# Branch products in source order on all queues, two low parts on GpSimd, and another plan of the attention

## The chip, the cores and the metric

The kernel runs on one core of a Trainium2 chip. A core has five engines with a queue each: TensorE (PE, matrix products; its weight loads appear as PEld), VectorE (DVE), ScalarE (ACT), GpSimd (POOL) and SyncE (SP, which only issues transfers). A queue is worked off in order, so an instruction that waits holds up all that stand behind it on its engine. The metric is the device time of one execution in microseconds, lower is better; 1533.11 us is the median of three runs of the kernel before.

## The reference

One layer over 1024 latent tokens (channels D = 1024) and 256 context tokens, in float32:

```python
mod = silu(c) @ w_mod + b_mod                 # six vectors: shift, scale, gate, twice
h = x * (1 + scale1) + shift1
proj = h @ w_in + b_in                        # q, k, v of branches A and B, and gate logits
o_a = windowed_attention(...)                 # 8 heads, +-128 tokens and the context, a sink per head
o_b = global_attention(...)                   # 8 heads, all 1280 keys, q and k normalized
g_a, g_b = split(sigmoid(gate_logits), 2)
y = (g_a * (o_a @ w_branch_a) + g_b * (o_b @ w_branch_b)) @ w_out
x = layer_norm(ALPHA * x + gate1 * y)
h = x * (1 + scale2) + shift2
y = conv_ffn(h)                               # up, depthwise convolution, silu, product, down
out = layer_norm(ALPHA * x + gate2 * y)
```

The change is in the attention's plan and in the line that makes `y` from `o_a` and `o_b`, up to the product with `w_out`.

## The kernel before

**Products in three parts.** Every large product is made from operands split into a high part (float32 rounded to the format fp32r) and a low part (what is left). `split` issues both: a copy, by default on ACT or POOL, and a subtraction on DVE or POOL. `mm3` issues three matmuls, high by high, high by low, low by high. In the profile these are lines 374 to 376, the copy on ACT is line 366 and the low part line 371. Tensors are held with channels on the 128 partitions and tokens along the row, in two halves of 512 tokens.

**Stages.** By the trace the projections and gates run to about 322 us, the attention from 322.7 to about 740, the rest of the branch products to 778.9, the product with w_out to 871, the FFN's up part to 1302 and its down part to 1522.

**Attention.** There are 32 units, one for each branch, block of 128 queries and group of four heads; unit 1_3_0 is branch 1 (global), block 3, group 0. A unit's steps: split and turn its queries (qs, qtr, q1), swap halves of them by a transfer (q2), scores (s), row maxima and scaling on DVE (L786), exponentials on ACT (L795), transposes of the probabilities by PE (tr, tiles pt, L840), their high and low parts, and the products with the values (av, L849), high part first and then low. A tile whose index is in `POOLED` is copied by ACT and split on POOL (ptr, hi L1213, lo L1224); the others are split by ACT and DVE (hi L1218, lo L1224). The reciprocal of the softmax sum takes its own way: one row is sent to DRAM (dn, L826) and read back in two transfers that spread it over the partitions (rb, L830). At the end of a unit ACT copies the product out of PSUM (ptra), POOL makes `up` and `ot` from it, multiplies by rb (`tt`, L1249) and splits the result into the attention output O (L866, L863).

**What sets the order.** `graph` makes a list of all these operations with the engine, a cost and a key each, and `plan` gives the order: at each step it takes, from the first `LOOK` of each engine's list, the operation that can start earliest by its account, where `SLACK` allows a later start for a smaller key. `COST` holds for each kind how long it holds the engine and when its result is there, `KEY` the places relative to the unit's number, `FILL` the place of products that fill PE between units: branch A's products (ptb), weight splits (wh, wl) and gate loads (sg). The source then issues each operation in that order, and the queues keep it, because the attention is written under a manual schedule.

Into the plan are also put sums of parts of w_dn that a transfer (sd, L878) and an accumulating transfer issued by POOL (L879) make, and the first halves of the branch B products of f = 0 to 3 (`grp`, with `bm` for the product with the gate).

**Branch products behind attention.** For f = 0 to 3, `rest` loads the second half of the gate, makes the product of the second half of the tokens (`group`, 12 matmuls, tile b, one of two small PSUM buffers `sml`) and multiplies it by the gate on DVE (`gmul`, L1115). For f = 4 to 7, `both` makes both halves (24 matmuls, one of three large buffers) and multiplies on DVE (L1392). `merge` adds branch A's and branch B's parts (DVE, L1372) and splits the sum into mh (ACT) and ml (DVE) for the product with w_out. The weights w_b of two f each are a block; blocks 0 and 1 are split in the plan, block 2 (rwb2, hwb2, lwb2) and block 3 behind it. `wout_start` loads w_out blocks (rwo, hwo, lwo) and the residual z, scaled on POOL (L1368). From the first of these products on, the order was set by a scheduler and not by the source.

Of the kernel before, what the change touches and what calls it, by code (L numbers as in the profile page):

```python
# [7 lines left out]
F32 = mybir.dt.float32  # L8
R32 = mybir.dt.float32r
AF = mybir.ActivationFunctionType  # L10
ALU = mybir.AluOpType
# [6 lines left out]
KT = 8  # L18
# [21 lines left out]
PWB = 5  # L40
DAH = 3
SINK = 640
POOLED, FILL, SUMS = ((0,), (1, 8)), (16.885703, 28.298765), ('ot1', 'ot1')
LOOK, SLACK = 24, (0, 0, 0.031835, 0.0879, 0.031696)
D3AT = (7, 5), (7, 9), (4, 1), (4, 4), (4, 7), (4, 10), (5, 2)
NXS = 5
RAWB = 3
# [38 lines left out]
def plan(ops, rings, free, look, slack):  # L86
# [5 lines left out]
    while any(todo):  # L92
# [25 lines left out]
        for b in o.uses:  # L118
# [25 lines left out]
PRING = "pt", "s", "av"  # L144
RINGS = dict(pt=3, s=2, av=1, qs=1, q1=2, q2=2, p=8, hi=4, lo=4, ptr=2, up=1, ot=1, rb=2, wraw=1, wh=1, wl=1)

KEY = {'qh': -1.21914, 'qt': -1.187093, 'sc': -0.106225, 'scs': (0.233244, 0.27861),
           'scx': -1.945172, 'tr': 0.840531, 'tru': (0.122743, 0.070723),
           'av': 1.36184, 'st': 1.192968, 'out': 0.661224, 'exd': 1.373419, 'st1': 1.769253, 'wb': (27.79832, 29.926055),
           'wg': (31.897283, 33.009176, 33.189585, 33.435465), 'ge': 0.762978, 'gr': 4.580045}  # L150
UNITS = 32


def graph(x, key=KEY, pooled=((3,), (2, 6)), fill=None, ot=("ot0", "ot1")):
    ops, last = [], {}
    def op(kind, k, fn, after=(), takes=(), uses=()):
        e, occ, lat = COST[kind]
        o = Op(e, kind, occ, lat, k, fn, after, takes, uses, kind in PORT)
        ops.append(o)
        return o  # L160
# [21 lines left out]
    for u in range(UNITS):  # L182
# [71 lines left out]
        r = op("rc", kn, lambda u=u, p=pt, b=rb: x.rc(u, p, b), [t], [rb], [pt])  # L254
        dn = op("dn", kn, lambda u=u: x.dn(u), [r], uses=[rb])
        rbd = op("rb", kn, lambda u=u: x.rb(u), [dn], uses=[rb])
        av = Buf("av")
        avo, trs = [], []
        for j, n in enumerate(kt):
# [61 lines left out]
    for f2 in (0, 1):  # L321
        raw = Buf("wraw")
        k = key["wb"][f2]
        a = op("ld", k, lambda f2=f2, r=raw: x.ld(4 + f2, r), [grps[-1]], [raw])
        b_ = op("wh", k + .1, lambda f2=f2, r=raw: x.wh(4 + f2, r, None), [a], uses=[raw])
        c = op("wl", k + .1, lambda f2=f2, r=raw: x.wl(4 + f2, r, None), [b_], uses=[raw])
        for n in (2 * f2, 2 * f2 + 1):
            pt = Buf("pt")
            d = op("sg", UNITS - 1 + .1 * n, lambda f=8 + n: x.sg(f, 0), end)
            e = op("grp", key["wg"][n], lambda f=8 + n, p=pt: x.grp(f, 0, p), [b_, c] + [units[u]["ol"] for u in range(16, 24)], [pt])  # L330
            op("bm", UNITS - .5 + .1 * n, lambda f=8 + n, p=pt: x.bm(f, 0, p), [e, d], uses=[pt])
    op("ld", UNITS - .6, lambda: x.rw(2), end)
    put = {}
    for u0, j0, j1 in ((17, 0, 4), (22, 4, 8), (25, 8, 11)):
# [17 lines left out]
def layer_kernel(  # L352
# [70 lines left out]
    def hput(*names):  # L423
        for n in names:
            hfree.append(hslot.pop(n))
# [686 lines left out]

    def gmul(br, f, hf):
        b = bT[br, f][:, hf * HALF:(hf + 1) * HALF]
        nc.vector.tensor_tensor(out=b, in0=bacc[br, f, hf], in1=b, op=ALU.mult)  # L1115
# [185 lines left out]
    pp.release()  # L1301
    qp.release()

    def rest(f, mk):
        gload(1, f, 1)
        group(1, f, 1, mk(f"b1_{f}_1"))
        gmul(1, f, 1)


    za = tc.alloc_tile_pool(name="za", bufs=1, side="right", reuse_waits="tile")  # L1310
    wq = tc.alloc_tile_pool(name="wq", bufs=1, side="right", reuse_waits="tile")
# [15 lines left out]
    def sml(name, w=512):  # L1327
        return ps3.tile([P, w], F32, tag="sml", name=name, bufs=2)
# [41 lines left out]
    def merge(f):  # L1370
        m = bT[0, f]
        nc.vector.tensor_tensor(out=m, in0=m, in1=bT[1, f], op=ALU.add)  # L1372
        mh, ml = ht(f"mh{f}", dt=R32), ht(f"ml{f}", dt=R32)
        split(m, mh, ml, nc.scalar, nc.vector)
        hput(f"bT0_{f}", f"bT1_{f}")
        mrg.append((mh, ml))

    wb = {2: [wq.tile([P, 8, P], R32, tag="w", name=f"{a}wb2", bufs=4) for a in "hl"]}
    split(rwb[2], *wb[2], nc.scalar, nc.vector)
    hput("rwb2")  # L1380

    def both(f):
        bT[1, f] = ht(f"bT1_{f}")
        nc.sync.dma_start(bT[1, f], sgd[KT + f])
        ps = big(f"b1_{f}")
        w = wb[f // 2]
        for hf in (0, 1):
            for j in range(4):
                k = (f % 2) * 4 + j
                a = O[1, hf, 0, j // 2][:, j % 2], O[1, hf, 1, j // 2][:, j % 2]  # L1390
                mm3(ps[:, hsl(hf)], (w[0][:, k], w[1][:, k]), a, j == 0, j == 3)
        nc.vector.tensor_tensor(out=bT[1, f], in0=ps, in1=bT[1, f], op=ALU.mult)  # L1392

    for f in range(KT):
        if f < 4:
            rest(f, sml)
        else:
            both(f)
        merge(f)
        if f == 3:  # L1400
            wb[3] = weight(w_b[3], "wb3", 8, he=nc.scalar, le=nc.vector, rtag=None)
        if f in (5, 7):
            wout_start(f // 2 - 2, None)
    opool.release()

    post = tc.alloc_tile_pool(name="post", bufs=1, side="left", reuse_waits="tile")
# [789 lines left out]
```

## Time and profile before

| what | value |
|---|---|
| median of the runs (lowest, highest) | 1533.11 us (1532.28, 1533.4) |
| profiled execution | 1533.52 us |
| its span | 1531.7 us |
| busy: PE, DVE, ACT, POOL | 1512.8, 1144.3, 801.2, 772.2 us |
| the largest waits of PE | branch products 4.4 us, attention's av 1.9 and 0.7 us |

A row of a timeline has the start, the duration, the engine, the line, the operation, the output and inputs, and in brackets how long the engine was idle just before and what ended that. SPq is SP's queue. A view of waits has, for each engine and line, what was waited for, the total, the number of times and the longest. Rows that belong to a helper have the helper's line, so the tile's name tells which of its calls it is. A matmul's row is longer than the time to the next, since matmuls are pipelined.

### The profile page before, as it was taken

Reading aid. Unit: us, or ns where it says so; the run is one execution under the profiler, and the core shown is the slowest. Engines: PE = TensorE matmul, PEld = TensorE weight load, DVE = VectorE, ACT = ScalarE, POOL = GpSimd, SP = SyncE. Lnnn points to the kernel's source line nnn. Section 1 sums busy time; section 2 is a strip of 40 time slices with the busy share of each in tenths; the row PEclk is TensorE's granted clock in tenths of the full one; section 3 lists DMA queues with packets and bytes.
Section 4 is the critical chain, followed back from the end, with each engine's and each line's share of the span. In section 5 each row is a group of like instructions: output and inputs, shape, how many; then the busy total and the mean of one; then the engine's idle time right before and its main releaser. Section 6 shows DMA issues by size and latency. Waiting matters only on the chain.

```text
span 1531.7 us, 21972 instructions
## 1 busy us (share of the span) xinstructions
PE 1512.8 (99%) x7652; PEld 1272.2 (83%) x7652; DVE 1144.3 (75%) x1729; ACT 801.2 (52%) x1403; POOL 772.2 (50%) x741
## 2 busy tenths in 40 slices
PE   9999999999999999999899999999999999999997
PEld 7888888889998887888788998888888888888886
DVE  7587847629777776787656898888887787656897
ACT  5422223448987776788232574444444444435533
POOL 0365303428896665685323546666676664021063
PEclk9999999999999999999999999999999999999999
DMA  9667663312445663732471223333344446996723
GB/s 377 235 234 254 212 240 111 97 38 67 118 117 145 174 153 94 161 98 70 139 165 35 96 92 109 110 111 112 111 104 110 110 112 183 377 274 213 247 84 110
DMA packets 112161, 229.73 MB, mean 150 GB/s; under 512 B 13521, under 2 KB 27345, under 8 KB 111954
## 3 DMA queue, kind: packets, MB, share of 16 engines
q1 hardware_dynamic: 97040, 199.72, 39.5%
q0 software_dynamic: 10400, 20.19, 8.6%
q10 hardware_dynamic: 4610, 8.42, 1.5%
q8 instruction: 60, 0.98, 0.3%
q14 instruction: 51, 0.42, 0.1%
HBM read 177.09 MB, written 65.87 MB: 159 GB/s over the span
## 4 chain that ended last, share of the span: by engine, by line
PE 92%; DVE 3%; DMA 1%; POOL 1%; issue 1%; ACT 1%; SPq 0%; DVEq 0%; POOLq 0%; ACTq 0%
PE av L849 7%; PE pt L840 6%; PE g L376 4%; PE g L374 4%; PE g L375 4%; PE p L375 3%; PE p L374 3%; PE p L376 3%; PE s L752 3%; PE s L753 3%; PE c L376 2%; PE d L376 2%; PE a L376 2%; PE d L375 2%; PE a L375 2%; PE c L375 2%
## 5 line engine op out<-in xcount | busy, mean ns | idle before, releaser
L1224 DVE TENSOR_TENSOR lo<-pt,hi 128x512 fp32r<-128x512 f32 x188 | 127.9, 688 | 53.0 <-ACT hi L1218 46.5
L371 DVE TENSOR_TENSOR ld<-rd,hd 128x1024 fp32r<-128x1024 f32 x77 | 97.6, 1285 | 49.2 <-ACT hd L366 47.1
L1218 ACT CAST hi<-pt 128x512 fp32r<-128x512 f32 x188 | 108.3, 582 | 39.9 <-PE pt L840 28.9
L366 ACT CAST hd<-rd 128x1024 fp32r<-128x1024 f32 x77 | 79.5, 1050 | 84.9 <-PE p L376 57.9
L374 PE MATMUL p<-hd 128*128 128x512 f32 x264 | 103.4, 392 | 0.0
L375 PE MATMUL p<-ld,hd 128*128 128x512 f32 x264 | 102.9, 390 | 0.4 <-DVE ld L371 0.4
L849 PE MATMUL av<-hi,VT 128*128 128x512 f32 x236 | 101.4, 431 | 1.9 <-POOL hi L1213 1.9
L376 PE MATMUL p<-hd,ld 128*128 128x512 f32 x264 | 102.9, 390 | 0.0
L849 PE MATMUL av<-lo,VT 128*128 128x512 f32 x236 | 101.8, 434 | 0.7 <-POOL lo L1224 0.7
L376 PE MATMUL g<-hh,wlg 128*128 128x512 f32 x256 | 99.8, 390 | 0.4 <-POOL wlg L371 0.4
L374 PE MATMUL g<-hh,whg 128*128 128x512 f32 x256 | 100.1, 391 | 0.0
L375 PE MATMUL g<-hl,whg 128*128 128x512 f32 x256 | 99.8, 390 | 0.0
L371 POOL TENSOR_TENSOR wlg<-wg,whg 128x512 fp32r<-128x512 f32 x32 | 45.1, 1416 | 106.2 <-ACT whg L366 89.1
L786 DVE TENSOR_SCALAR_CACHE_REDUCE p<-s,cvt,nmc 128x1024 f32<-128x1024 f32 x64 | 85.6, 1337 | 5.6 <-PE s L753 5.3
L840 PEld LDWEIGHTS pt<-ident,p 128*128 128x128 f32 x512 | 63.5, 140 | 17.2 <-ACT rb L822 0.4
L795 ACT ACTIVATE p<-p,nm 128x1024 f32<-128x1024 f32 x64 | 73.9, 1154 | 6.2 <-DVE p L786 5.8
L840 PE MATMUL pt<-ident,p 128*128 128x128 f32 x512 | 76.7, 272 | 0.1
L752 PE MATMUL s<-KL,q 128*128 128x512 f32 (+2 forms) x186 | 74.1, 398 | 0.0
L366 ACT CAST wS<-s 128x512 fp32r<-128x512 f32 x76 | 45.3, 621 | 55.1 <-POOL s L1528 54.3
L753 PE MATMUL s<-KL,q 128*128 128x512 f32 (+2 forms) x186 | 69.7, 374 | 0.0
L371 DVE TENSOR_TENSOR wS<-s,wS 128x512 fp32r<-128x512 f32 x57 | 53.5, 966 | 16.6 <-ACT wS L366 16.6
L366 ACT CAST wA<-ru 128x512 fp32r<-128x512 f32 x57 | 35.5, 623 | 57.7 <-PE d L376 28.8
(436 smaller groups left out, 5026.4 us busy)
## 6 DMA issues: line engine op xcount, KB each, us to landing
wml<-in_wmodT_dram SPq DMA_DIRECT2D x48, 512.0 KB
ru<-in_w_up_dram SPq DMA_DIRECT2D x38, 512.0 KB
rd<-td SPq DMA_DIRECT2D x55, 256.0 KB
rd<-sd SPq DMA_DIRECT2D x44, 256.0 KB
rd<-in_w_dn_dram SPq DMA_DIRECT2D x33, 256.0 KB
wm<-in_wmodT_dram SPq DMA_DIRECT2D x16, 512.0 KB
wg<-in_w_g_dram SPq DMA_DIRECT2D x32, 256.0 KB
q<-q SPq DMA_DIRECT2D x64, 128.0 KB
```

The source lines that it names most:

```text
L366: cast[:] = [nc.scalar.copy(hi, src).ins]
L371: low[:] = [lo_eng.tensor_tensor(out=lo, in0=src, in1=hi.bitcast(F32), op=ALU.subtract).ins]
L374: nc.tensor.matmul(ps, a[0], b[0], start=start, stop=False, skip_group_check=resumed)
L375: nc.tensor.matmul(ps, a[0], b[1], start=False, stop=False, skip_group_check=resumed)
L376: return nc.tensor.matmul(ps, a[1], b[0], start=False, stop=stop, skip_group_check=resumed).ins
L752: nc.tensor.matmul(o, self.q1[:, hs], ks, start=True, stop=False)
L753: nc.tensor.matmul(o, self.q2[:, hs], ks, start=False, stop=stop)
L786: nc.vector.tensor_scalar(out=p if self.br else p[:, self.pad + 1:SINK + 1], in0=self.sv[h], scalar1=self.scale()[:, hs] if self.br else - ...
L840: nc.tensor.transpose(tr[:, h * P:(h + 1) * P], src, ident)
L849: nc.tensor.matmul(self.av, v, self.parts[n][low], start=first, stop=self.left == 0)
L1218: nc.scalar.copy(hi, units[u].parts[n])
L1224: e.tensor_tensor(out=lo, in0=src, in1=hi.bitcast(F32), op=ALU.subtract)
```

## The change

It has two parts.

The plan gets other numbers: `KEY`, `FILL`, `SLACK` (all zero now), tile 6 in place of tile 8 of a global unit on POOL, and a longer time for the reciprocals' way back. The loads of the second halves of branch B's gates for f = 0 to 3 become operations of the plan.

The branch products behind the attention are put under the manual schedule of all five queues, in another source order: the low parts of weight blocks 2 and 3 go to POOL, the low part of a merge is issued one step later (`msplit`), the gate loads of f = 4 to 7 are issued ahead (`later`), block 3 is loaded and split at f = 1, and w_out's first blocks are started ahead of the gate product of f = 5 and 7. Lines of the attention's functions move by two, so L1115 becomes L1117.

```diff
-POOLED, FILL, SUMS = ((0,), (1, 8)), (16.885703, 28.298765), ('ot1', 'ot1')
-LOOK, SLACK = 24, (0, 0, 0.031835, 0.0879, 0.031696)
+POOLED, FILL, SUMS = ((0,), (1, 6)), (16.988136, 27.931), ('ot1', 'ot1')
+LOOK, SLACK = 24, (0, 0, 0, 0, 0)
...
-KEY = {'qh': -1.21914, 'qt': -1.187093, 'sc': -0.106225, 'scs': (0.233244, 0.27861),
+KEY = {'qh': -0.919337, 'qt': -1.197497, 'sc': -0.139853, 'scs': (0.199825, 0.270357),
...
         rbd = op("rb", kn, lambda u=u: x.rb(u), [dn], uses=[rb])
+        rbd.lat = 6.0 if 17 <= u < 30 else 4.2
...
             op("bm", UNITS - .5 + .1 * n, lambda f=8 + n, p=pt: x.bm(f, 0, p), [e, d], uses=[pt])
+            op("sg", UNITS - .5 + .1 * n, lambda f=8 + n: x.sg(f, 1), end)
...
-    def rest(f, mk):
-        gload(1, f, 1)
-        group(1, f, 1, mk(f"b1_{f}_1"))
-        gmul(1, f, 1)
...
         mh, ml = ht(f"mh{f}", dt=R32), ht(f"ml{f}", dt=R32)
-        split(m, mh, ml, nc.scalar, nc.vector)
+        nc.scalar.copy(mh, m)
+        mrg.append((mh, ml))
+
+    def msplit(f):
+        mh, ml = mrg[f]
+        nc.vector.tensor_tensor(out=ml, in0=bT[0, f], in1=mh.bitcast(F32), op=ALU.subtract)
         hput(f"bT0_{f}", f"bT1_{f}")
-        mrg.append((mh, ml))
 
     wb = {2: [wq.tile([P, 8, P], R32, tag="w", name=f"{a}wb2", bufs=4) for a in "hl"]}
-    split(rwb[2], *wb[2], nc.scalar, nc.vector)
+    branch = ExitStack()
+    branch.enter_context(tc.manual_schedule(engines={mybir.EngineType.PE, mybir.EngineType.DVE, mybir.EngineType.SP,
+                                                     mybir.EngineType.Activation, mybir.EngineType.Pool}))
+    split(rwb[2], *wb[2], nc.scalar, nc.gpsimd)
     hput("rwb2")
 
     def both(f):
-        bT[1, f] = ht(f"bT1_{f}")
-        nc.sync.dma_start(bT[1, f], sgd[KT + f])
         ps = big(f"b1_{f}")
...
-        nc.vector.tensor_tensor(out=bT[1, f], in0=ps, in1=bT[1, f], op=ALU.mult)
-
+        return ps
+
+    def later(f):
+        bT[1, f] = ht(f"bT1_{f}")
+        nc.sync.dma_start(bT[1, f], sgd[KT + f])
+
+    for f in (4, 5):
+        later(f)
     for f in range(KT):
         if f < 4:
-            rest(f, sml)
+            group(1, f, 1, sml(f"b1_{f}_1"))
+            gmul(1, f, 1)
+            if f:
+                msplit(f - 1)
+            if f == 1:
+                wb[3] = weight(w_b[3], "wb3", 8, he=nc.scalar, le=nc.gpsimd, rtag=None)
+            if f == 3:
+                later(6)
+                later(7)
         else:
-            both(f)
+            ps = both(f)
+            msplit(f - 1)
+            if f in (5, 7):
+                wout_start(f // 2 - 2, None)
+            nc.vector.tensor_tensor(out=bT[1, f], in0=ps, in1=bT[1, f], op=ALU.mult)
         merge(f)
-        if f == 3:
-            wb[3] = weight(w_b[3], "wb3", 8, he=nc.scalar, le=nc.vector, rtag=None)
-        if f in (5, 7):
-            wout_start(f // 2 - 2, None)
+    msplit(KT - 1)
+    branch.close()
```

Three places show what the queues hold. First DVE from the last gate product inside the plan (ptb11_0) on, before; b1_0_1 is the second half of the branch B product of f = 0, bT0_0 and bT1_0 the parts of branch A and B, and the number at a name's end only tells buffers apart:

```order
L1115 TENSOR_TENSOR bT1_3_8404<-ptb11_0_8591,bT1_3_8404 128x512
L371 TENSOR_TENSOR lwb3_8715<-rwb3_8712,hwb3_8714 128x1024
L1115 TENSOR_TENSOR bT1_0_8370<-b1_0_1_8633,bT1_0_8370 128x512
L1372 TENSOR_TENSOR bT0_0_4909<-bT0_0_4909,bT1_0_8370 128x1024
L371 TENSOR_TENSOR lwo0_8787<-rwo0_8784,hwo0_8786 128x1024
L371 TENSOR_TENSOR ml0_8649<-bT0_0_4909,mh0_8648 128x1024
L1115 TENSOR_TENSOR bT1_1_8381<-b1_1_1_8653,bT1_1_8381 128x512
```

and after, from the same gate product on:

```order
L1117 TENSOR_TENSOR bT1_3_8402<-ptb11_0_8598,bT1_3_8402 128x512
L1117 TENSOR_TENSOR bT1_0_8367<-b1_0_1_8642,bT1_0_8367 128x512
L1369 TENSOR_TENSOR bT0_0_4903<-bT0_0_4903,bT1_0_8367 128x1024
L1117 TENSOR_TENSOR bT1_1_8375<-b1_1_1_8660,bT1_1_8375 128x512
L1376 TENSOR_TENSOR ml0_8658<-bT0_0_4903,mh0_8657 128x1024
L1369 TENSOR_TENSOR bT0_1_4925<-bT0_1_4925,bT1_1_8375 128x1024
L1117 TENSOR_TENSOR bT1_2_8386<-b1_2_1_8685,bT1_2_8386 128x512
```

The low parts lwb3 and lwo0 are gone from between the gate products, and ml0 stands behind the second gate product instead of ahead of it.

Second POOL at the end of unit 1_3_0, before; hi1_3_1_1 and lo1_3_1_1 are the parts of pooled tile 1 of the next unit:

```order
L1242 TENSOR_SCALAR up1_3_0_6741<-ptra1_3_0_6737 64x512
L854 TENSOR_TENSOR ot1_3_0_6746<-ptra1_3_0_6737,up1_3_0_6741 64x256 x2
L1249 TENSOR_TENSOR ot1_3_0_6746<-ot1_3_0_6746,rb1_3_0_6674 128x256
L1213 TENSOR_SCALAR hi1_3_1_1_6769<-ptr1_3_1_1_6761 128x512
L866 TENSOR_SCALAR O1000_5403<-ot1_3_0_6746 128x2x128
L1224 TENSOR_TENSOR lo1_3_1_1_6783<-ptr1_3_1_1_6761,hi1_3_1_1_6769 128x512
L863 TENSOR_TENSOR O1010_5414<-ot1_3_0_6746,O1000_5403 128x2x128
```

and after:

```order
L1215 TENSOR_SCALAR hi1_3_1_1_6763<-ptr1_3_1_1_6747 128x512
L1244 TENSOR_SCALAR up1_3_0_6767<-ptra1_3_0_6754 64x512
L1226 TENSOR_TENSOR lo1_3_1_1_6777<-ptr1_3_1_1_6747,hi1_3_1_1_6763 128x512
L856 TENSOR_TENSOR ot1_3_0_6791<-ptra1_3_0_6754,up1_3_0_6767 64x256 x2
L1251 TENSOR_TENSOR ot1_3_0_6791<-ot1_3_0_6791,rb1_3_0_6670 128x256
L868 TENSOR_SCALAR O1000_5456<-ot1_3_0_6791 128x2x128
L865 TENSOR_TENSOR O1010_5459<-ot1_3_0_6791,O1000_5456 128x2x128
L1215 TENSOR_SCALAR hi1_3_1_6_6841<-ptr1_3_1_6_6826 128x512
L1226 TENSOR_TENSOR lo1_3_1_6_6860<-ptr1_3_1_6_6826,hi1_3_1_6_6841 128x512
```

Tile 1 moved from behind the multiply with rb1_3_0 to ahead of it, and the second pooled tile, now 6, stands right behind the unit's outputs.

Third ACT at the end of the branch products, before; mh6 and mh7 are the high parts of the last merges, hwo1 to hwo3 those of w_out blocks:

```order
L366 CAST hwo1_8864<-rwo1_8862 128x1024
L366 CAST mh3_8708<-bT0_3_5020 128x1024
L366 CAST mh4_8747<-bT0_4_5039 128x1024
L366 CAST mh5_8780<-bT0_5_5160 128x1024
L366 CAST mh6_8825<-bT0_6_5520 128x1024
L366 CAST mh7_8858<-bT0_7_5832 128x1024
L366 CAST hwo2_8889<-rwo2_8887 128x1024
```

and after:

```order
L1371 CAST mh4_8755<-bT0_4_5045 128x1024
L368 CAST hwo0_8786<-rwo0_8784 128x1024
L1371 CAST mh5_8798<-bT0_5_5058 128x1024
L1371 CAST mh6_8829<-bT0_6_5361 128x1024
L368 CAST hwo1_8860<-rwo1_8858 128x1024
L368 CAST hwo2_8892<-rwo2_8890 128x1024
L1371 CAST mh7_8872<-bT0_7_5724 128x1024
```

The high part hwo2 moved from behind mh7 to ahead of it; on DVE lwo2 stands ahead of ml7 in the same way.

More of the change, by code (lines that the diff above doesn't have):

```diff
@@ L145 @@
 RINGS = dict(pt=3, s=2, av=1, qs=1, q1=2, q2=2, p=8, hi=4, lo=4, ptr=2, up=1, ot=1, rb=2, wraw=1, wh=1, wl=1)
-KEY = {'qh': -1.21914, 'qt': -1.187093, 'sc': -0.106225, 'scs': (0.233244, 0.27861),
-           'scx': -1.945172, 'tr': 0.840531, 'tru': (0.122743, 0.070723),
-           'av': 1.36184, 'st': 1.192968, 'out': 0.661224, 'exd': 1.373419, 'st1': 1.769253, 'wb': (27.79832, 29.926055),
-           'wg': (31.897283, 33.009176, 33.189585, 33.435465), 'ge': 0.762978, 'gr': 4.580045}
+KEY = {'qh': -0.919337, 'qt': -1.197497, 'sc': -0.139853, 'scs': (0.199825, 0.270357),
+           'scx': -3.142963, 'tr': 0.868828, 'tru': (0.216182, 0.070723),
+           'av': 1.348883, 'st': 1.265771, 'out': 0.885708, 'exd': 1.273589, 'st1': 1.664154, 'wb': (27.969376, 29.459582),
+           'wg': (31.81419, 33.291489, 33.170198, 33.528645), 'ge': -0.046198, 'gr': 4.26668}
 UNITS = 32
```

## The prediction

> **What bounds the kernel now.** I read the page's busy shares first, then the view of what the tensor engine waited for, then the timelines of the engines around its long waits. The page says that TensorE does the work of nearly the whole span:
>
> ```profile
> PE   1512.8 (99%) x7652; PEld 1272.2 (83%) x7652; DVE 1144.3 (75%) x1729; ACT 801.2 (52%) x1403; POOL 772.2 (50%) x741
> ```
>
> ```profile
> PE b L374 <- DVE bT L1115: 4.4, 2, 2.6
> PE av L849 <- POOL hi L1213: 1.9, 2, 1.7
> PE av L849 <- POOL lo L1224: 0.7, 1, 0.7
> ```
>
> The matmuls themselves stay the same, so only waits can be won. The second fence gives total, number and longest of a wait. Two lie in the branch products (b), the rest in attention (av). Both places by the timelines of PE, first the branch products and the undisturbed steps behind them:
>
> ```profile
> 747.04 0.50 PE L374 MATMUL b<-O,hwb 128*128 128x512 f32 x1 [1.81 <-DVE bT L1115]
> 747.38 0.40 PE L375 MATMUL b<-O,hwb 128*128 128x512 f32 x1
> ...
> 753.10 0.50 PE L374 MATMUL b<-O,hwb 128*128 128x512 f32 x1 [2.59 <-DVE bT L1115]
> 753.44 0.49 PE L375 MATMUL b<-O,hwb 128*128 128x512 f32 x1
> 753.73 0.63 PE L376 MATMUL b<-O,lwb 128*128 128x512 f32 x1
> 754.15 0.63 PE L374 MATMUL b<-O,hwb 128*128 128x512 f32 x1
> ...
> 757.08 0.40 PE L375 MATMUL b<-O,hwb 128*128 128x512 f32 x1
> ...
> 778.64 0.39 PE L376 MATMUL b<-O,lwb 128*128 128x512 f32 x1
> 778.87 0.39 PE L374 MATMUL y<-mh,hwo 128*128 128x512 f32 x1
> ```
>
> An undisturbed matmul starts 0.23 us after the one ahead of it (778.64 to 778.87; over long rows 0.227). After the wait of 2.59 us the ten steps from 753.10 to 757.08 take 3.98 us where ten steps take 2.27: 1.71 us more, and the view by windows shows the granted clock at 0.72 there (first column behind POOL's):
>
> ```profile
> 752.00:758.00 6.00, 4.90 (x14) 3.88 (x15) 5.62 (x7) 2.09 (x2) 1.54 (x2) 0.72 0.58 171
> ```
>
> Who was late is told by the other engines:
>
> ```profile
> 740.42 0.34 SPq L1336 DMA_DIRECT2D rwb<-in_w_b_dram  x1
> ...
> 744.08 1.05 ACT L366 CAST hwb<-rwb 128x1024 fp32r<-128x1024 f32 x1 [8.10 <-DMA rwb<-in_w_b_dram]
> ...
> 745.16 1.23 DVE L371 TENSOR_TENSOR lwb<-rwb,hwb 128x1024 fp32r<-128x1024 f32 x1 [4.64 <-ACT hwb L366]
> 746.31 0.68 DVE L1115 TENSOR_TENSOR bT<-b,bT 128x512 f32<-128x512 f32 x1
> 747.02 1.23 DVE L1372 TENSOR_TENSOR bT<-bT,bT 128x1024 f32<-128x1024 f32 x1
> 749.49 1.41 DVE L371 TENSOR_TENSOR lwo<-rwo,hwo 128x1024 fp32r<-128x1024 f32 x1 [1.24 <-ACT hwo L366]
> 750.82 1.63 DVE L371 TENSOR_TENSOR ml<-bT,mh 128x1024 fp32r<-128x1024 f32 x1
> 752.37 1.28 DVE L1115 TENSOR_TENSOR bT<-b,bT 128x512 f32<-128x512 f32 x2
> ...
> 749.21 2.17 POOL L1368 TENSOR_SCALAR z<-z 128x512 f32<-128x512 f32 x2 [8.81 <-DMA z<-in_xT_dram]
> ```
>
> These are rows of SP, ACT, DVE and POOL. The gate multiply of f = 0 (746.31) frees the small PSUM buffer for which the third group waits; it stands on DVE behind the low part of weight block 3, which waits for ACT's high part and that for a load issued at 740.42. The multiply of f = 1 (752.37) stands behind the low parts of the first w_out block and of the merge. POOL has nothing to do for 8.81 us.
>
> In attention, rows of POOL, SP and PE:
>
> ```profile
> 584.76 1.17 POOL L879 DMA_DIRECT2D sd<-in_w_dn_dram  x1
> ...
> 588.27 1.35 SPq L830 DMA_DIRECT2D rb<-dn  x2
> ...
> 595.99 0.72 POOL L1249 TENSOR_TENSOR ot<-ot,rb 128x256 f32<-128x256 f32 x1 [3.49 <-DMA rb<-dn]
> 596.68 0.62 POOL L1213 TENSOR_SCALAR hi<-ptr 128x512 fp32r<-128x512 f32 x1
> ...
> 597.63 1.26 POOL L1224 TENSOR_TENSOR lo<-ptr,hi 128x512 fp32r<-128x512 f32 x1
> ...
> 597.35 0.50 PE L849 MATMUL av<-hi,VT 128*128 128x512 f32 x1 [1.73 <-POOL hi L1213]
> ...
> 598.95 0.50 PE L849 MATMUL av<-lo,VT 128*128 128x512 f32 x1 [0.66 <-POOL lo L1224]
> ```
>
> The reciprocals of unit 1_3_0 were sent at 588.27 and their multiply could start at 595.99, over 7 us later, beside an accumulating DMA issued at 584.76. The pooled tile of the next unit stood behind that multiply on POOL, and PE waited 1.73 and 0.66 us for it.
>
> **The change part by part.**
>
> Branch products. Low parts of weight blocks 2 and 3 go from DVE to POOL; the low part of each merge stands one step later on DVE; w_out's low parts stand behind the merges of f = 4 and on. DVE then has per early step a multiply, a merge and a low part, 0.68 + 1.23 + 1.23 = 3.14 us, against a PE group of 12 x 0.227 = 2.72. Counted from the start T of the first group: its multiply ends at T + 3.4, the merge at T + 4.6, the second multiply (group ready at T + 5.45) at T + 6.1. The third group wants the first buffer at T + 5.45, the fourth the second at T + 8.2. So 2.0 us are left at both. With merge and low part at the 1.63 us of the row at 750.82 the second multiply is still done by T + 6.1. The later products use the large buffers. Both waits go: −1.81 − 2.59 = −4.40. With them the slow steps, −1.71, and the late step behind the first wait (747.04 to 747.38 instead of 0.23), −0.11. Together −6.2.
>
> The price on POOL: the low part of such a block there has rows in attention, and the widest spread of POOL's low parts is in the row of wA (min, median, max in ns), half its size:
>
> ```profile
> L1269 POOL TENSOR_TENSOR lwb<-wraw,hwb x2: 2372/2384/2397, 658.8 to 677.5; 128x1024 fp32r<-128x1024 f32 x2
> L371 POOL TENSOR_TENSOR wA<-ru,wA x19: 1288/2269/2277, 941.5 to 1289.1; 128x512 fp32r<-128x512 f32 x19
> ```
>
> So 2.4 to 4.6 us. Block 2 stands behind POOL's last attention output, which ended near 740.4: done by 742.8 to 745.0, wanted with f = 4 at T + 10.9, near 750.4 with T near 739.5. Block 3 stands behind two scalings of z (749.21 and 2.17 us): done by 753.8 to 756.0, wanted with f = 6 at T + 21.8, near 761.3. I take nothing for either; the cover is 5 us, and if z's loads come 5 us later it is gone and each us more is a us of PE. The load of block 3 moves ahead on SP, behind the last reciprocals; it waits for a late attention product, and nothing of attention is queued behind it. Next on SP stand the gate loads of f = 6 and 7, which wait for the last attention output, and then w_out's and z's. z was issued here before:
>
> ```profile
> 742.28 1.03 SPq L1367 DMA_DIRECT2D z<-in_xT_dram  x2
> ```
>
> The output that they now wait for is done near 740.4 at the latest, so z leaves about as before. The second halves of the gates of f = 0 to 3 stay ahead of the last transfers, as they were: nothing. The loads for f = 4 and 5 now stand ahead of the last unit's two transfers on SP and wait for old attention tiles; the reciprocals have nearly 12 us of room there (sent 725.42, used 737.49):
>
> ```profile
> 725.42 1.22 SPq L830 DMA_DIRECT2D rb<-dn  x2
> 737.49 0.73 POOL L1249 TENSOR_TENSOR ot<-ot,rb 128x256 f32<-128x256 f32 x1
> ```
>
> Two new neighbours at the end of the stage. On ACT the high part of w_out block 2 now stands ahead of that of the last merge, and on DVE its low part ahead of ml7. Its load was issued only when the branch products had ended:
>
> ```profile
> 779.78 1.98 SPq L1336 DMA_DIRECT2D rwo<-in_w_out_dram  x3
> ...
> 784.51 1.05 ACT L366 CAST hwo<-rwo 128x1024 fp32r<-128x1024 f32 x1 [1.49 <-DMA rwo<-in_w_out_dram]
> ...
> 783.05 1.23 DVE L371 TENSOR_TENSOR ml<-bT,mh 128x1024 fp32r<-128x1024 f32 x1 [1.12 <-ACT mh L366]
> ```
>
> Before, ml7 was done at 784.3, which is 5.4 us after y's start at 778.87. Now: ACT's cast ends 6.7 us after y's start, mh7 7.75, DVE's low part of the block 8.0, ml7 9.2. The first matmul with ml7 is the 41st of y, 40 x 0.227 = 9.1 us after the start. That is +0.1 by these rows, and one to one with the landing of that load: 0 to +1, I take +0.3.
>
> Attention. The plan's new numbers move no instruction from one engine to another except that tile 6 of a global unit is pooled in place of tile 8. At unit 1_3_0 the pooled tile 1 of 1_3_1 now stands ahead of the multiply with the reciprocals: −1.73 − 0.66 and two late steps of 0.1 each, −2.6. The transfer out and the one back in stand next to each other on SP in every unit, and the accumulating DMAs are issued at other places, mostly just ahead of a multiply. The planner now reckons 6.0 us for the way back of the reciprocals in units 17 to 29 and 4.2 elsewhere, in place of 3.1; the 7.7 us from 588.27 to 595.99 are nearer to the new figure, which is why I expect the waits to be fewer and not only elsewhere. What new waits come I can only bound: nothing, or all that POOL waited for reciprocals (total and times, from the view of the transfer's line):
>
> ```profile
> POOL ot L1249: 14.0, 6
> ```
>
> Six waits of 14.0 us, of which one reached PE, with 2.4. Nearest is that five of six stayed hidden, so I take +0.3 and keep 0 and +14. The tail of the plan has one more group of weight block 10 or 9 behind the last attention product, which starts the last output chain earlier: nothing on PE, since the groups only change place.
>
> A rule of the Trainium skill, TensorE: Matmul & The Clock Gate, Part 1: an idle window of about 3.4 us brings the array to half its clock, and cold matmuls of 512 columns start 426.7 ns apart. The trace agrees with the step (753.73 to 754.15 is 0.42 us), but not with the length, for the wait was 2.59 us. By the page the wait alone would not slow the clock, and the sum would keep those 1.7 us.
>
> Sum against the profiled execution (1533.5 us: span 1531.7 and 1.8 around it): −6.2 + 0.3 − 2.6 + 0.3 = −8.2, 1525.3. The median of the runs is 0.4 lower, so 1525.
>
> **The rivals.**
>
> First, the attention part is a trade: the wait at 597 goes and others of the same total come, for every unit has another order. Then −5.9 alone, up to +3 for waits: 1527 to 1530. For it: 16 global units with new neighbours. Against it: the one long wait has one cause, and the new order removes it.
>
> Second, on the other side: the reciprocals late at many units, now with tile 6 behind them. On POOL that tile's high and low part stand right behind the multiply and the two outputs of the unit ahead. In most global units 24 to 36 matmul steps lie between the transposes of tile 6 and its product, 5.4 to 8.2 us; a multiply 3.5 us late leaves POOL 1.3 + 0.6 + the outputs 1.1 to do and may pass that. If all the 14.0 us reached PE the time would be 1525 + 14 = 1539. It decides from 11.2 us on, over four waits like that at 597. Against it: in all of attention before, such waits reached PE once, and tile 1, the nearest to its use, moved ahead of the multiply.
>
> Third, the slow steps were not due to the wait and come again: 1525 + 1.7 = 1526.7. For it: the wait of 1.73 us at 597 is followed by steps of the usual length. Against it: the clock fell just behind the longest wait.
>
> Fourth, the edit does not do what it says, since POOL's low part of block 3 waits for z: 1 to 5 us of PE before f = 6, 1526 to 1530. The row at 749.21 leaves 5 us of cover, so this is held within the first.
>
> **How the numbers follow.** A measurement of this kernel can tell about 0.2%, 3.1 us, from no change: 1530.0 to 1536.2 counts as the same. The forecast with its own range of 1522.3 to 1527 has 0.57: its low end is −6.2 − 2.6 with the 0.2 of other av waits, 1524.1, less 0.8 for the spread of runs and 1 for waits too short for the view. The third rival has 0.05, the first with the fourth 0.20 up to 1530 and 0.09 between 1530 and 1536 (waits of 5 to 11 us), the second 0.09. Faster 0.82, same 0.09, slower 0.09. The range goes from 1522.3 to 1531.5, leaving out the second rival, most of the 0.09 beside it and a little below.
>
> **What would show it.** Right: no wait of b on bT in the branch stage, its PE row without a gap from the first group to y, granted clock 1.00 there, DVE's multiply of f = 1 right behind the first merge; no wait of av on POOL of over half a us; ml7 close to its use. Wrong: PE waiting for av's hi or lo from POOL at several units behind a multiply that waits for rb; PE waiting for lwb from POOL, or for ml7 by more than a us; the steps behind small waits at 0.42 us.

## The result, and the profile after

The changed kernel takes 1526.54 us (median of 6 runs, 1525.27 to 1529.23) against 1533.32 us (6 runs, 1532.28 to 1534.1): a ratio of 0.9958 with a 95% interval of 0.9945 to 0.9971, faster by 0.4%. The forecast was 1525.0, in a range of 1522.3 to 1531.5. The profiled execution of the changed kernel took 1527.93 us, with a span of 1526.1; that is 1.4 above the median, and 5.6 below the profiled execution before.

The waits of TensorE after, by engine and line (total, times, longest):

```profile
PE y L377 <- DVE ml L1376: 1.4, 1, 1.4
...
PE y L376 <- ACT mh L1371: 1.0, 1, 1.0
PE p L377 <- DVE ld L373: 0.9, 1, 0.9
...
PE y L378 <- DVE lwo L373: 0.3, 1, 0.3
...
PE av L851 <- POOL hi L1215: 0.2, 1, 0.2
```

No product b waits any more, and av's waits on POOL are down to 0.2 us. New ones stand at y, the product with w_out. Where the time went shows best by the starts of the stages. The first b of the kernel before, of the one after, and the first y after:

```profile
739.63 0.39 PE L374 MATMUL b<-O,hwb 128*128 128x512 f32 x1
```

```profile
735.68 0.39 PE L376 MATMUL b<-O,hwb 128*128 128x512 f32 x1
...
768.32 0.39 PE L376 MATMUL y<-mh,hwo 128*128 128x512 f32 x1
```

Up to the first b 3.95 us were won. The branch stage, from the first b to the first y, takes 32.6 us in place of 39.2, 6.6 won; y started at 778.87 before, so it stands 10.55 us earlier. The view by windows has y's stage at 92.7 us before and 96.3 after:

```profile
778.90:871.60 92.70, 92.70 (x509) 80.42 (x508) 61.27 (x79) 35.53 (x51) 35.78 (x26) 1.00 0.36 93
```

```profile
768.30:864.60 96.30, 93.56 (x509) 80.23 (x507) 64.46 (x82) 37.27 (x52) 36.40 (x26) 1.00 0.34 94
```

3.6 us were given back there, and 1.4 more behind it, of which the wait for ld (0.9, above; it was 0.4 before) is a part. The balance is −3.95 − 6.6 + 3.6 + 1.4 = −5.6.

What happened at y shows in rows of PE, SP, ACT and DVE of the changed kernel:

```profile
779.00 0.50 PE L376 MATMUL y<-mh,hwo 128*128 128x512 f32 x1 [1.05 <-ACT mh L1371]
780.86 0.50 PE L377 MATMUL y<-ml,hwo 128*128 128x512 f32 x1 [1.36 <-DVE ml L1376]
...
769.79 0.96 SPq L1364 DMA_DIRECT2D z<-in_xT_dram  x2
771.17 0.80 SPq L1333 DMA_DIRECT2D rwo<-in_w_out_dram  x2
...
776.95 1.05 ACT L368 CAST hwo<-rwo 128x1024 fp32r<-128x1024 f32 x1 [5.10 <-DMA rwo<-in_w_out_dram]
777.90 1.04 ACT L1371 CAST mh<-bT 128x1024 fp32r<-128x1024 f32 x1
...
768.53 1.23 DVE L1369 TENSOR_TENSOR bT<-bT,bT 128x1024 f32<-128x1024 f32 x1
...
774.46 1.64 DVE L1369 TENSOR_TENSOR bT<-bT,bT 128x1024 f32<-128x1024 f32 x1
778.03 1.23 DVE L373 TENSOR_TENSOR lwo<-rwo,hwo 128x1024 fp32r<-128x1024 f32 x1 [1.93 <-ACT hwo L368]
779.18 1.63 DVE L1376 TENSOR_TENSOR ml<-bT,mh 128x1024 fp32r<-128x1024 f32 x1
```

The last merge is done at 776.1 and mh7 could be cast then. ACT stands at the cast of w_out's block 2, whose load was issued at 771.17, 2.85 us after y's start, and arrived 5.8 us later. mh7 and ml7 stand behind it. That load stands on SP behind the load of z at 769.79, and z waited for the merge of f = 6, which ended at 769.76 (DVE's row at 768.53). SP's waits between 766 and 772 us:

```profile
SPq L1364 <- DVE bT L1369: 6.6, 1, 6.6
```

In attention, POOL at the place of the old wait, after:

```profile
591.74 0.62 POOL L1215 TENSOR_SCALAR hi<-ptr 128x512 fp32r<-128x512 f32 x1 [4.91 <-ACT ptr L1210]
592.44 0.61 POOL L1244 TENSOR_SCALAR up<-ptra 64x512 f32<-64x512 f32 x1
593.14 1.30 POOL L1226 TENSOR_TENSOR lo<-ptr,hi 128x512 fp32r<-128x512 f32 x1
594.39 1.54 POOL L856 TENSOR_TENSOR ot<-ptra,up 64x256 f32<-64x256 f32 x2
596.01 0.74 POOL L1251 TENSOR_TENSOR ot<-ot,rb 128x256 f32<-128x256 f32 x1
```

Tile 1's parts come first, and the multiply at 596.01 doesn't wait for its reciprocals. Over the whole attention POOL now waits once for them (from the view of the transfer's line), where it was six times with 14.0 us:

```profile
POOL ot L1251: 1.8, 1
```

### The profile page after: what moved, and what is told of

It reads as the page before. It is cut to its first block, busy times and chain, and to the rows that moved or that the text cites. A ratio compares the mean times of both kernels' runs of the same rounds, so it can differ in the third digit from the quotient of the medians.

```text
span 1526.1 us, 21981 instructions
## 1 busy us (share of the span) xinstructions
PE 1510.1 (99%) x7652; PEld 1269.0 (83%) x7652; DVE 1146.5 (75%) x1727; ACT 799.2 (52%) x1403; POOL 779.4 (51%) x743
## 4 chain that ended last, share of the span: by engine, by line
PE 90%; DVE 4%; DMA 2%; POOL 1%; issue 1%; ACT 1%; SPq 0%; DVEq 0%; POOLq 0%; ACTq 0%
PE av L851 7%; PE pt L842 6%; PE g L378 4%; PE g L377 4%; PE g L376 4%; PE p L377 3%; PE p L378 3%; PE p L376 3%; PE s L754 3%; PE s L755 3%; PE c L377 2%; PE d L377 2%; PE a L377 2%; PE c L376 2%; PE d L376 2%; PE a L376 2%
## 5 line engine op out<-in xcount | busy, mean ns | idle before, releaser
L788 DVE TENSOR_SCALAR_CACHE_REDUCE pa<-s,negsink 128x640 f32<-128x640 f32 (+1 forms) x58 | 49.3, 853 | 29.2 <-PE s L755 28.7
```

The costliest lines, as they stand in the source:

```text
L788: nc.vector.tensor_scalar(out=p if self.br else p[:, self.pad + 1:SINK + 1], in0=self.sv[h], scalar1=self.scale()[:, hs] if self.br else - ...
```

## The experiments

Each ratio is against executions of the kernel before that were run beside the experiment; their medians lie between 1532.80 and 1533.18 us.

**The plan alone.** The kernel before with the new numbers of the plan.

```diff
 # before.py with after.py's POOLED, FILL, SLACK and KEY, and
+        rbd.lat = 6.0 if 17 <= u < 30 else 4.2
```

> The plan's new numbers alone; the branch products as before, under the scheduler. My theory: the attention gains by itself what it gains in the whole change, its excess over undisturbed steps falls from 6.9 to about 2.9 us and the first product b starts some 4 us earlier. The branch stage keeps its waits on bT; as the scheduler here puts the low parts of weight block 3 and of the first w_out block both ahead of the first gate product on DVE, I expect one wait of 5 to 7 us there in place of 4.4, with slow steps behind it. Sum -4 + 1 to 3: 1530 to 1532. Rival: the attention's gain needs the new branch stage (through the loads that moved); then b starts at the old time and the sum is 1534 to 1536.

1527.66 us, ratio 0.9966 (0.9949 to 0.9983), below the 1530 to 1532 that I expected. The first b starts at 735.38, against 735.68 in the whole change, so the attention's gain is the plan's own. The branch stage was less bad than I expected, 37.8 us, with one wait on the gate product:

```profile
744.19 0.50 PE L375 MATMUL b<-O,hwb 128*128 128x512 f32 x1 [3.21 <-DVE bT L1116]
...
745.73 0.63 PE L377 MATMUL b<-O,lwb 128*128 128x512 f32 x1
746.16 0.63 PE L375 MATMUL b<-O,hwb 128*128 128x512 f32 x1
```

```profile
742.00:748.00 6.00, 3.81 (x11) 3.00 (x12) 5.83 (x6) 1.56 (x3) 4.07 (x4) 0.76 0.39 147
```

Behind this single wait the slow steps of 0.43 us come again, 0.8 us after its end, with the granted clock at 0.76 (second fence, a window of 6 us, the clock behind POOL's column).

**The branch stage alone.** The changed kernel with the old plan's numbers.

```diff
 # after.py with before.py's POOLED, FILL, SLACK and KEY, and
-        rbd.lat = 6.0 if 17 <= u < 30 else 4.2
```

> The new branch stage alone, with the old plan's numbers. My theory: the wait at 597 us stays (1.7 and 0.7 us), the branch stage loses its 6.6 us, and the product with w_out waits for mh7 and ml7 as in the changed kernel (2.7 us and some): 1533.3 - 6.6 + 3.4 = 1530.1. Rival: the waits for mh7 and ml7 come from the new plan, whose tail ends otherwise; then they are under 0.5 us here and the sum is 1527.

1532.51 us, ratio 0.9993 (0.9983 to 1.0004): no difference that can be measured, where I had expected 1530.1, though its profiled execution, at 1528.48, shows a branch stage of 32.6 us and a wait of only 0.8 us at ml7. The old wait at 597 us is there:

```profile
597.77 0.50 PE L850 MATMUL av<-hi,VT 128*128 128x512 f32 x1 [2.15 <-POOL hi L1214]
...
599.37 0.51 PE L850 MATMUL av<-lo,VT 128*128 128x512 f32 x1 [0.66 <-POOL lo L1225]
```

A wait of 2.15 us, and behind it no lower clock: the granted clock from 596 to 603 us is 1.00.

**The same once more**, to see an execution near the median.

> A second look at the new branch stage with the old plan, whose profiled execution was 4 us faster than its median. If the 4 us are waits for mh7 and ml7, an execution near 1532 shows them as 3 us or more at the start of the product with w_out, with slow steps behind, and the landing of w_out's block 2 later than the 4.9 us behind its issue in the first profile; if they are the attention's, the wait at 597 us is over 3 us.

The one execution took 1527.35 us, with 0.7 us at ml7 and 1.9 at 597. It was again a good one, so what the longer executions of this kernel lose was not seen in a profile.

**w_out's block 2 behind the last merge.** This changes the order on ACT and DVE, and on SP.

```diff
     msplit(KT - 1)
-    branch.close()
...
+    for a in (2, 3):
+        wout_start(a)
+    branch.close()
...
     for f in range(0, KT, 2):
-        if f + 2 < KT:
+        if f and f + 2 < KT:
```

> The changed kernel with w_out's blocks 2 and 3 split behind the last merge on ACT and DVE (mh7, ml7 first). Theory one: the waits of the product with w_out have two causes, the order of block 2 ahead of mh7, and DVE being late by then (the last merge ends 7.8 us after that product's start, where the first matmul with ml7 comes 9.1 after it). Then mh7 is in time, ml7 is late by about 1 us, the wait for the low part of block 1 (0.3) stays: waits 1.3 in place of 2.7, 1525.1. Theory two: block 2's load alone: waits 0.3, 1524.1.

1524.46 us, ratio 0.9943 (0.9928 to 0.9958). The view of waits has none of PE from the first b to the end of y's stage, and that stage takes 93.4 us:

```profile
769.20:862.60 93.40, 93.40 (x509) 80.40 (x509) 65.35 (x88) 37.82 (x53) 39.20 (x28) 1.00 0.37 102
```

Theory two holds: the order, and with it the landing of one load, is the cause of the waits at y. The median is 2.1 us below that of the changed kernel, though the two intervals still overlap (0.9945 to 0.9958). Theory one was not far off, for ml7 comes without any reserve. It ends at 778.20, and the 41st matmul of y, which reads it, starts 0.33 us after the one ahead of it in place of 0.23, as the end of ml7 lets it:

```profile
768.78 0.39 PE L376 MATMUL y<-mh,hwo 128*128 128x512 f32 x1
...
777.93 0.39 PE L376 MATMUL y<-mh,hwo 128*128 128x512 f32 x1
778.26 0.50 PE L377 MATMUL y<-ml,hwo 128*128 128x512 f32 x1
...
776.90 1.30 DVE L1376 TENSOR_TENSOR ml<-bT,mh 128x1024 fp32r<-128x1024 f32 x1 [1.12 <-ACT mh L1371]
```

**The gate product ahead of the merge's low part on DVE.**

```diff
             ps = both(f)
+            nc.vector.tensor_tensor(out=bT[1, f], in0=ps, in1=bT[1, f], op=ALU.mult)
             msplit(f - 1)
             if f in (5, 7):
                 wout_start(f // 2 - 2, None)
-            nc.vector.tensor_tensor(out=bT[1, f], in0=ps, in1=bT[1, f], op=ALU.mult)
```

> The changed kernel with the gate product of f = 4 to 7 ahead of the low part of the merge before it on DVE, so that DVE doesn't idle for ACT's high part. Theory one (two causes): DVE's idle times of 1.1 us behind each merge go and the last merge ends 2 us or more earlier, but ml7 still stands behind block 2's low part, done near 780.4: the waits for mh7 and ml7 stay near 2.4 us, the 0.3 for the low part of block 1 goes: 1526. Rival (DVE's lateness alone): the waits go, 1523.8.

1525.31 us, ratio 0.9946 (0.9929 to 0.9962), an interval that overlaps with the changed kernel's. DVE no longer idles for ACT's high part behind the merges of f = 4 to 6, but PE still waits 1.0 us for ml7, because block 2's low part stands ahead of it:

```profile
776.03 1.23 DVE L373 TENSOR_TENSOR lwo<-rwo,hwo 128x1024 fp32r<-128x1024 f32 x1 [2.07 <-ACT hwo L368]
...
777.67 1.21 DVE L1376 TENSOR_TENSOR ml<-bT,mh 128x1024 fp32r<-128x1024 f32 x1
```

An earlier DVE alone doesn't remove the wait, as the rival, DVE's lateness alone, would have it.

**All orders together**, both edits above and w_out's block 1 one step earlier.

```diff
-            if f in (5, 7):
-                wout_start(f // 2 - 2, None)
+            if f in (5, 6):
+                wout_start(f - 5, None)
```

> The changed kernel with w_out's blocks 2 and 3 behind the last merge, the gate product of f = 4 to 7 ahead of the low part of the merge before it, and w_out's block 1 started at f = 6. My theory: with the order of block 2 alone PE waited nowhere from the first branch product on, but ml7 was done 8.9 us after the start of the product with w_out, where 9.1 is its limit. Here it is done some 3 us earlier; no PE wait is left to win, so the time is that of the kernel with block 2 behind, within 1 us: 1524 to 1525, with less spread between runs. Rival: the small reserve costs in some executions, and the median falls by 1 us or more to 1523.

1523.18 us (1522.04 to 1524.36), ratio 0.9937 (0.9924 to 0.9949). It is the fastest of all; its slowest execution is below the fastest of the changed kernel (1525.27). Its interval overlaps with that of block 2's order alone, so whether the reserve at ml7 brings anything is not settled. The 8.9 us that I gave for ml7 with block 2 behind were misread: by the rows above it ended 9.4 us after y's start (768.78 to 778.20), so there was no reserve left.

**The branch stage alone, with block 2 behind.**

```diff
 # the branch stage alone (old plan), and
     msplit(KT - 1)
-    branch.close()
...
+    for a in (2, 3):
+        wout_start(a)
+    branch.close()
```

> The old plan with the new branch stage and w_out's blocks 2 and 3 behind the last merge. The branch stage alone took 32.6 us in its profile (39.3 before), and yet its median was within 0.1% of the kernel before, the profiled execution being 4 us faster than the median. Theory one: the 4 us are waits for mh7 and ml7 of a size that changes from run to run with the landing of block 2; they are gone here, and the time is 1533 - 6.6 = 1526.5. Theory two: the 4 us are the attention's wait at 597 us, with slow steps behind it in most executions; then the time stays near 1531.

1528.08 us, ratio 0.997 (0.9956 to 0.9984), 4.4 us below the branch stage alone. So the 4 us hang on the order of block 2, since nothing else was changed; that they are a longer wait at y in those executions, with slow steps behind it, is the likely reading, but only argued. The mean granted clocks on record fit slow steps: 0.997 to 0.999 in the four shortest of the ten executions without the edit, 0.995 to 0.997 in the six longest, and 0.997 or 0.998 in nine of the ten with it; a difference of 0.002 over 1530 us is some 3 us by my estimate. They don't tell where in the kernel the steps are. The time stays 1.6 us above the 1526.5 that I expected.

**The low parts on DVE again**, in the kernel with block 2 behind.

```diff
-    split(rwb[2], *wb[2], nc.scalar, nc.gpsimd)
+    split(rwb[2], *wb[2], nc.scalar, nc.vector)
...
-                wb[3] = weight(w_b[3], "wb3", 8, he=nc.scalar, le=nc.gpsimd, rtag=None)
+                wb[3] = weight(w_b[3], "wb3", 8, he=nc.scalar, le=nc.vector, rtag=None)
```

> The changed kernel with w_out's block 2 behind the last merge and the low parts of weight blocks 2 and 3 on DVE again, in the new source order. Theory: the gain of the branch stage comes from the order and the earlier load of block 3 and not from GpSimd: DVE has 1.2 us more, but isn't held by GpSimd's low part of 2.4 us (ml1 took 2.74 us beside it in place of 1.23), so the low part of f = 7 comes as late as with GpSimd or earlier, and the time is the same as with block 2 behind: 1524.5, no wait of b. Rival: DVE is the bound there and 1.2 us more make ml7 late: a wait of about 1 us at mh7 and ml7, 1525.5 to 1526.

1524.69 us, ratio 0.9947 (0.9932 to 0.9963), against 1524.46 with GpSimd: the same. The branch stage has no wait of PE. So with block 2 behind, the move to GpSimd that the title names brings nothing by itself. What is left of the branch stage's change, the order and the earlier load of block 3, brings the gain; no run separates these two.

**The accumulating transfers left out** of the kernel before. The w_dn sums miss their second terms, so this only tells about the attention.

```diff
-            wab.pop(("sd", key, j0))()
+            wab.pop(("sd", key, j0))
```

> The kernel before with the accumulating transfers of the w_dn sums left out (the sums then miss their second term; nothing else changes its place). Theory: what makes the reciprocals late in units of branch B is that the transfers lie beside an accumulating one of 1 MB; without them the two transfers back land about 2.7 us after their issue as in branch A, POOL's 14.0 us of waits for rb fall under 2, and the waits at 597 us (1.7 and 0.7) go. Rival: the transfers are late because of the swaps of queries ahead of them on the same queue; then they land 7 us after issue here too and the wait stays.

1529.98 us in one execution, beside 1532.86 before. POOL's waits for reciprocals fall to 2.1 us (second fence), and at unit 1_3_0 the multiply at 591.71 no longer waits for the transfers, which were issued at 587.40:

```profile
587.40 1.29 SPq L830 DMA_DIRECT2D rb<-dn  x2
...
591.71 0.73 POOL L1249 TENSOR_TENSOR ot<-ot,rb 128x256 f32<-128x256 f32 x1
592.41 0.61 POOL L1213 TENSOR_SCALAR hi<-ptr 128x512 fp32r<-128x512 f32 x1
```

```profile
POOL ot L1249: 2.1, 2
```

The swaps of queries ahead on the queue are still there, so the rival is out: at this unit the accumulating transfer makes the reciprocals late. One of the two waits that are left stands beside plain transfers of 1 MB for the same sums, issued at 515.30 and 519.30: there the multiply started at 523.67, 5.7 us after the reciprocals were sent at 517.96. So a late return needs no accumulating transfer.

**The longer way alone.** The planner's time for the reciprocals' way back, in the kernel before.

```diff
         rbd = op("rb", kn, lambda u=u: x.rb(u), [dn], uses=[rb])
+        rbd.lat = 6.0 if 17 <= u < 30 else 4.2
```

> The kernel before with the longer time for the reciprocals' way back in the planner and nothing else. By the order this changes one place in the whole program: at unit 1_3_0 POOL's high and low part of the next unit's tile 1 stand ahead of the multiply with the reciprocals. Theory: the waits at 597 us (1.7 and 0.7 with two late steps, 2.6 in sum) are due to that place alone, and go: attention's excess 6.9 to about 4.2, the time 1530.2. Rival: the multiply still waits for the late transfers, and what stands behind it now (the outputs, tile 8) makes PE wait in its turn: excess over 6, no change of time.

1528.97 us, ratio 0.9966 (0.9956 to 0.9977), 4.2 us faster by one change of place on POOL:

```profile
592.43 0.62 POOL L1214 TENSOR_SCALAR hi<-ptr 128x512 fp32r<-128x512 f32 x1 [0.77 <-POOL ot L855]
593.13 1.30 POOL L1225 TENSOR_TENSOR lo<-ptr,hi 128x512 fp32r<-128x512 f32 x1
595.08 0.73 POOL L1250 TENSOR_TENSOR ot<-ot,rb 128x256 f32<-128x256 f32 x1 [0.66 <-DMA rb<-dn]
```

The multiply still waits for late transfers, but nothing that PE needs soon is behind it. In the profile the first b stands at 736.00, 3.6 earlier, of which 0.5 lies ahead of the attention (first scores at 322.16 in place of 322.69); the medians are 4.2 apart, so a part of the gain is not in that profile. In the changed kernel the same line does nothing: without it, the new `KEY` gives the same order on all five queues.

**The longer way with the new branch stage**, old numbers otherwise, block 2 behind.

```diff
 # the branch stage alone with block 2 behind, and
+        rbd.lat = 6.0 if 17 <= u < 30 else 4.2
```

> The old plan with the longer time for the reciprocals, the new branch stage, and w_out's blocks 2 and 3 behind the last merge: 1528.1 (the same without the longer time) less 2.6 to 3 by the one place on POOL: 1525.3. If the other new numbers of the plan bring what the profiles show (excess 2.9 against 4.2 and the earlier end of the last unit), this stays 1 us behind the kernel with all of them (1524.5); if it is the same or lower, those numbers bring nothing.

1523.95 us, ratio 0.9939 (0.9924 to 0.9954). With all new numbers and block 2 behind it was 1524.46: the other numbers of the plan bring nothing that shows in the time. The gains add up, 4.2 for the place on POOL and 4.8 for the branch stage with block 2 behind, against 9.2 here.

**Tile 8 in place of tile 6** in the changed kernel.

```diff
-POOLED, FILL, SUMS = ((0,), (1, 6)), (16.988136, 27.931), ('ot1', 'ot1')
+POOLED, FILL, SUMS = ((0,), (1, 8)), (16.988136, 27.931), ('ot1', 'ot1')
```

> The changed kernel with tile 8 pooled in place of tile 6, all other numbers new. My prediction's rival held that tile 6 behind the multiply could make PE wait. If the place of the second pooled tile matters, attention's excess differs from the 2.9 us of the changed kernel by more than 1; if the reciprocals are simply in time now, it is within 0.5 either way, and the time between 1525 and 1529.

1528.38 us in one execution. The first b is at 736.45, 0.8 us later than with tile 6, though the first scores came 0.6 us earlier (321.60 in place of 322.19): the attention took 1.4 us longer, more than the 1 us that I had set as a sign that the place matters. Between 680 and 710 us PE was idle for 0.3 us, 0.2 of it a wait of av on POOL's low part; where the rest lies isn't shown. One execution can't settle so small a difference; tile 6 behind the multiply is at least not the burden that I feared.

At y this execution shows more. PE waited there a little less than in the changed kernel's profile (0.74 and 1.36 us in place of 1.05 and 1.36), and yet slow steps followed, which that profile doesn't have; the granted clock was 0.72 between 780 and 786 us:

```profile
778.92 0.50 PE L376 MATMUL y<-mh,hwo 128*128 128x512 f32 x1 [0.74 <-ACT mh L1371]
780.79 0.50 PE L377 MATMUL y<-ml,hwo 128*128 128x512 f32 x1 [1.36 <-DVE ml L1376]
...
782.45 0.63 PE L377 MATMUL y<-ml,hwo 128*128 128x512 f32 x1
782.87 0.63 PE L378 MATMUL y<-mh,lwo 128*128 128x512 f32 x1
```

```profile
780.00:786.00 6.00, 5.21 (x16) 4.16 (x17) 5.47 (x6) 2.21 (x3) 1.62 (x2) 0.72 0.73 221
```

The nine steps from 782.05 to 785.70 took 3.65 us in place of 2.04. So waits of much the same size can cost 1.6 us more in one execution than in another.

## Why the prediction was right

The direction and the two large terms held: −6.8 us by the medians, −8.2 forecast. That the number came so near is in part luck. By the profiles the change is −5.6: the attention up to the first b gave 1.65 us more than its −2.3, the branch stage 0.4 more than its −6.2, y's stage cost 3.3 more than its +0.3, and 1.4 behind y was in no term. These misses have opposite signs and partly cancel. One of my own signs of being wrong came true as well, for PE waited 1.4 us for ml7 where I had set one us.

*Branch products, −6.2.* 6.6 were measured. Both waits and the slow steps are gone, and DVE's second multiply (741.32) ended 6.3 us after the first group's start at 735.68, where the step said 6.1. The rows of DVE and POOL there:

```profile
741.32 0.69 DVE L1117 TENSOR_TENSOR bT<-b,bT 128x512 f32<-128x512 f32 x1 [0.77 <-PE b L378]
...
745.89 2.74 DVE L1376 TENSOR_TENSOR ml<-bT,mh 128x1024 fp32r<-128x1024 f32 x1 [0.59 <-ACT mh L1371]
...
745.15 2.41 POOL L373 TENSOR_TENSOR lwb<-rwb,hwb 128x1024 fp32r<-128x1024 f32 x1
```

"I take nothing" for the low parts on POOL was right for PE, and the doubt about z was not needed (block 3 done at 747.6). But DVE paid for it: the low part ml1 took 2.74 us beside POOL's, over twice the 1.23 that it took with the low parts on DVE again. My 1.63 was too small a bound for that.

*W_out's block 2, "0 to +1, I take +0.3".* This is the step that failed, by its size: 2.4 us of waits for mh7 and ml7, 0.3 for the low part of block 1, and with the late steps around them 3.6 in the stage. The mechanism was named, and the experiment with block 2 behind takes it away. What I mis-sized is the landing of its load: I took issue and landing from the row of before, 0.9 and 5.6 us after y's start, and they became 2.85 and 8.6. About 1.9 us of that are the later issue, since on SP the load now stands behind a load of z that waits for the merge of f = 6; the rest is a longer way from issue to landing, 5.8 us in place of 4.7, for which I have no cause. I had counted who stands behind block 2 on ACT and DVE, but not what stands ahead of its load on SP.

*Attention, −2.6 + 0.3.* 3.95 us were won up to the first b, about 0.5 of it already ahead of the attention. The term was right in its place and cause (the longer way alone moves just that one multiply, and takes the wait away), and too small: with that one move the attention took 3.1 us less in its profile, where I had 2.6 for it, and why is open. Its account of new waits (+0.3) was not needed; that the rest of the plan's numbers would bring nothing, I had not seen.

*The rivals.* No wait of av on POOL is over 0.2 us, so the second, reciprocals late at many units with PE behind them, didn't come; POOL itself waited for them once, 1.8 us. The third, that the branch stage's slow steps are not due to its wait, is out: the new stage has none, and in the plan alone they came behind a wait of 3.2. The first, a trade in the attention, is out by the plan alone. The fourth, block 3 late on POOL, is out with its end at 747.6.

## What to carry to other kernels

A wait on the bounding engine that ends with an in-order engine's row is first a matter of what stands ahead of that row: here one place on POOL and the order of the branch stage, with block 2 behind, were worth some 9 us, and which engine makes the low parts nothing. When a step is moved ahead on an engine, follow its input back to the queue that loads it and re-derive the issue from what is ahead there, instead of taking it from the old row. Where a region under a hand-written order ends, the scheduler may still put later work in front of its last rows; close it behind the work that competes for them.

## What the hardware showed that I had not expected

GpSimd's subtraction with two inputs in SBUF holds up such an instruction of VectorE for nearly all the time that they overlap. In the changed kernel ml1 overlaps for 1.67 us with a POOL row of 2.41 and took 2.74 us; without a POOL row beside it (the low parts on DVE again) it took 1.23. With the longer way and the new branch stage the overlap is 2.25 us, and ml1 took 3.33:

```profile
746.03 3.33 DVE L1376 TENSOR_TENSOR ml<-bT,mh 128x1024 fp32r<-128x1024 f32 x1 [0.57 <-POOL z L1365]
745.89 2.39 POOL L373 TENSOR_TENSOR lwb<-rwb,hwb 128x1024 fp32r<-128x1024 f32 x1
```

The Trainium skill, GPSIMD Engine Reference, section 1, says that the interfaces are shared and in contention with VectorE instructions that have two SBUF inputs; the trace agrees.

TensorE's steps went to 0.43 us behind waits of 2.59 and 3.21 us (2.79 and 2.71 without the accumulation and with the longer way alone), and stayed at 0.23 behind waits of 1.73, 1.81 and 2.15. That looks like a length from which the clock falls, but the length of the wait doesn't decide alone: with tile 8 the steps went to 0.43 us behind waits of 0.74 and 1.36 us, and in the changed kernel they stayed at 0.23 behind 1.05 and 1.36 at the same place. In the execution with the low parts on DVE again, seven steps of 0.43 us come in the FFN's down part, behind 2.1 us of matmuls of one column (from 1454.84 on) with a single wait of 0.3 us among them:

```profile
1457.91 0.63 PE L376 MATMUL p<-hd 128*128 128x512 f32 x1
1458.33 0.63 PE L377 MATMUL p<-ld,hd 128*128 128x512 f32 x1
```

With block 2 behind alone, 1.7 us of such matmuls at the same place have no slow steps behind them. What decides isn't shown. The Trainium skill, TensorE: Matmul & The Clock Gate, part 1, speaks of an idle window of about 3.4 us; all the waits named here are shorter than that, so the traces don't agree with it as a length of one wait.

The reciprocals of unit 1_3_0 come back in two transfers of 64 KB. Beside an accumulating transfer of 1 MB they could be used 7.7 us after the first was issued (588.27 to 595.99); with the accumulating transfers left out, 4.3 us at the latest (587.40 to 591.71).
